# A hybrid encoder on one core: epsilon inside the sums of squares, a polish of two VectorE operations, one product per head norm, and another split of the last outputs

## The chip, the cores and the metric

The kernel runs on one core of a Trainium2 chip. The metric is the device time of one execution in microseconds: the median of three runs for the kernel before. The profile shows one further execution. Engines are named as in the profile: PE (TensorE matmul), DVE (VectorE), ACT (ScalarE), POOL (GpSimd), SP (the queue that issues DMAs).

## What is computed

One batch of 1024 tokens of width 1024 goes through four residual layers: attention (windowed heads of group A and full, RMS-normed heads of group B), an MLP, a spatial gating layer, an MLP, and a last RMSNorm. Every norm of it is of one kind, and those are what the change is about:

```python
def _rmsnorm(x, g):
    xf = x.astype(jnp.float32)
    y = xf * lax.rsqrt(jnp.mean(xf * xf, axis=-1, keepdims=True) + EPS)   # EPS = 1e-6
    return (y * g.astype(jnp.float32)).astype(x.dtype)

# group B of the attention layer: a norm over the 64 elements of a head
qb = _apply_axial_rope(_rmsnorm(qb, qn_g), cos_r, sin_r, cos_c, sin_c)
kb = _apply_axial_rope(_rmsnorm(kb, kn_g), cos_r, sin_r, cos_c, sin_c)
...
def _mlp(x, norm_g, w1, w2):
    h = _rmsnorm(x, norm_g)
    return x + jnp.square(jax.nn.relu(h @ w1)) @ w2
...
return _rmsnorm(h, final_norm)
```

## The kernel before

Activations lie transposed: 128 features on the partitions, tokens along the free axis, in two halves of 512 (`HN`). A tile `x[k][:, half]` is 128x512. Each fp32 product is three products of high and low parts (`mm3`, L268 to 270); the products of statistics (`ones`, `blk32`) are plain fp32 and show as two rows each. Both MLPs use a scheme of seven products for four (`product`, `up_step`), whose partial sums are put together from the PSUM banks by DVE (`r`, `u`, `ub`, `ua`).

A norm goes in four steps. ACT squares each x tile and POOL adds the squares up (`add_sq`, L311 to 314). PE adds over the partitions with a matrix of ones (`ssb`). ACT gives a first estimate of the inverse root: Ln and Exp (L321, L322) in the attention and the first MLP, one Abs_reciprocal_sqrt (L324) later. DVE polishes it by one Newton step: L325 makes the mean plus eps, L329 to L331 do the step. So a polish is four DVE operations. The activations are not scaled by it ahead of the products: `z` (L902) applies it to the finished `up` sums, and the attention applies it behind its projection.

The heads of group B have their own norm, inside `rotate` (L422 to 463), which is called for the key heads and for two sets of query heads, each for two halves: three normed calls a half, six in all. DVE does the four products of the rotation (L428, L430), ACT squares the two source banks (L433, L434), POOL subtracts and adds (L435, L436). The rest is a generator, `chain`, put into the list `chains`. `tick()` advances each generator of the list by one `yield`, and `lin`, the input projection, calls it after each k step, that is after twelve products. In the chain PE adds the squares over each head with two products by `blk32` (tile `hss`), DVE makes `ha` (L448), ACT does Ln and Exp into `hy`, DVE polishes with three operations (L329 to L331) and scales the rotated heads (L456), which are then split and stored to DRAM (`qs`, L461).

The last norm (`final`) runs for the whole first half, and for the second half in two quarters of 256 tokens, `rest` set. In the second half the last tile of x to be finished is x[3]: its `dz` products come last, DVE adds them (L1087), and `done` squares the tile (L1000). Each of the eight output tiles of a quarter is either scaled on DVE in one operation (L1113), or on ACT by the weight (L1110) and on POOL by rstd (L1111). Every third tile (`k % 3 == 2`: tiles 2 and 5) goes the second way. SP issues the output DMAs in the order of k.

A scheduler sets the order on each engine from the order in which the program emits its instructions, with pins (`in_turn`) that keep some behind the last product. Tiles of 128x512 come from a ring of twelve buffers (`tr` and `nr`, pool `trp`); a tile's first writer waits for the last reader of the tile that had the buffer before. PSUM has eight banks (`psp`).

Of the kernel before, what the change touches and what calls it, by code (L numbers as in the profile page):

```python
# [7 lines left out]
F32 = mybir.dt.float32  # L8
# [5 lines left out]
P = 128  # L14
# [18 lines left out]
def tile_kernel(ctx: ExitStack, tc: tile.TileContext, I, out, upto=99, dbg=None):  # L33
# [54 lines left out]
    par = const("par", [P, N_PAR])  # L88
    eps = cp.tile([P, 1], F32, name="eps")
    dve.memset(eps, EPS)  # L90
    ones = cp.tile([P, P], F32, name="ones")
# [213 lines left out]
    def add_sq(k, half, xs, w_=HN):  # L305
        if (half, "n") not in sumsq:
            a = nr("ss")
            act.activation(a[:, 0:w_], xs, AF.Square)
            sumsq[half, "n"] = 1
            sumsq[half] = a  # L310
        else:  # L311
            t = tr("sq")[:, 0:w_]
            act.activation(t, xs, AF.Square)  # L313
            pool.tensor_tensor(sumsq[half][:, 0:w_], sumsq[half][:, 0:w_], t, op=ALU.add)  # L314

    rsq = ["exp"]

    def rsqrt0(y0, a, s, scale):

        if rsq[0] == "exp":  # L320
            act.activation(y0, s, AF.Ln, scale=scale, bias=eps)  # L321
            act.activation(y0, y0, AF.Exp, scale=-0.5)  # L322
        else:
            act.activation(y0, s, AF.Abs_reciprocal_sqrt, scale=scale, bias=eps)  # L324
        dve.tensor_scalar(a, s, scale, EPS, op0=ALU.mult, op1=ALU.add)  # L325

    def newton(y0, a, dst):

        dve.tensor_tensor(a, y0, a, op=ALU.mult)  # L329
        dve.scalar_tensor_tensor(a, a, -0.5, y0, op0=ALU.mult, op1=ALU.mult)  # L330
        dve.scalar_tensor_tensor(dst, a, 1.5, y0, op0=ALU.add, op1=ALU.mult)  # L331

    def rstd_rows(half):

        s = ps("ssb")
        mm(s, ones, sumsq[half], True, True)
        y0, a = tr("y0"), tr("va")
        rsqrt0(y0, a, s, 1.0 / D)
        r = nr("rstd")
        newton(y0, a, r)  # L340
        return r

    def rstd_cols(half):

        s = ps("ssc")
        for tb in range(4):
            mm(s[:, tb : tb + 1], sumsq[half][:, tb * P : (tb + 1) * P], ones[:, 0:1], True, True)
        y0, a = sm("rc_y", [P, 4]), sm("rc_a", [P, 4])
        rsqrt0(y0, a, s[:, 0:4], 1.0 / D)
        r = sm("rc_r", [P, 4])  # L350
        newton(y0, a, r)
        return r
# [57 lines left out]
    def att_rstd(half):  # L410
# [4 lines left out]
        rsqrt0(y0, a, s, 1.0 / D)  # L415
        dve.tensor_scalar(evb[:, half], s, EPS / D, EPS * EPS, op0=ALU.mult, op1=ALU.add)
        rst[half] = rstb[:, half]
        newton(y0, a, rst[half])

    ready = {}  # L420

    def rotate(key, half, p1, p2, C, S, c1=None, c2=None, late=0):  # L422
# [8 lines left out]
        if c1 is not None:  # L431
            s1, s2 = tr("s1"), tr("s2")
            act.activation(s1, p1, AF.Square)  # L433
            act.activation(s2, p2, AF.Square)  # L434
        pool.tensor_tensor(de[:, 0], de[:, 0], w1, op=ALU.subtract)  # L435
        pool.tensor_tensor(de[:, 1], de[:, 1], w2, op=ALU.add)  # L436

        def chain():
            for _ in range(1 + late):
                yield 1  # L440
            if c1 is not None:
                s = ps("hss")
                mm(s, blk32, s1, True, False)
                mm(s, blk32, s2, False, True)
                yield 1
                y0, a = tr("hy"), tr("ha")

                dve.scalar_tensor_tensor(a, s, 1.0 / 64.0, evb[:, half], op0=ALU.mult, op1=ALU.add)  # L448
                act.activation(y0, a, AF.Ln)
                act.activation(y0, y0, AF.Exp, scale=-0.5)  # L450
                yield 1
                newton(y0, a, a)
                if key == "k":
# [638 lines left out]
    def final(half, a, b, rest):  # L1092
# [11 lines left out]
        r = nr("rstd")[:, 0:w_]  # L1104
        newton(y0, va, r)
        for k in range(KT):
            xs = x[k][:, half, a:b]
            o = tr("o")[:, 0:w_]
            if k % 3 == 2:
                act.activation(o, xs, AF.Copy, scale=col(C_FIN + k))  # L1110
# [266 lines left out]
```

## Time and profile before

| | us |
|---|---|
| median of 3 runs (lowest to highest) | 2071.59 (2068.70 to 2072.35) |
| the profiled execution | 2072.43 |
| its span from first to last instruction | 2070.7 |
| PE busy in it | 2027.1 (98%) |
| DVE busy | 1457.3 (70%) |
| ACT busy | 961.8 (46%) |
| POOL busy | 568.6 (27%) |

A row of a timeline gives the start and the length in us of one instruction or of several of a kind in a run (x6: six), its engine, the line, what it writes and reads, and in brackets how long the engine stood idle just ahead of it and which instruction ended that. Instructions in a pipeline overlap a little, so a row can be longer than the step to the next one. A releaser is inferred from the semaphores; of several it is the one that came last.

### The profile page before, as it was taken

The page shows a single profiled execution, that of the slowest core. Times are in us where ns is not written, and L with a number is a line of the kernel's source. Part 1 is how long each engine was busy: PE and PEld are TensorE (multiplying, and loading weights), DVE is VectorE, ACT ScalarE, POOL GpSimd, SP SyncE. Part 2 cuts the span into 40 slices and gives each one's busy share as a digit, 9 for nine tenths or more (in the row PEclk, how much of TensorE's full clock was granted, in tenths as well). Part 3 has the DMA queues.
Part 4 walks back from the last instruction along what each step waited for, and adds up shares of the span by engine and source line. Part 5 has one row for each costly group of instructions (what it writes and reads, how often), then busy time and mean ns, then how long its engine had stood idle before and what let it go on. Part 6 is the DMA issues. An engine that isn't in the chain of part 4 may idle for free.

```text
span 2070.7 us, 27136 instructions
## 1 busy us (share of the span) xinstructions
PE 2027.1 (98%) x9162; PEld 1672.5 (81%) x9162; DVE 1457.3 (70%) x2322; ACT 961.8 (46%) x1765; POOL 568.6 (27%) x440
## 2 busy tenths in 40 slices
PE   8998999999999999999999999999999999999997
PEld 7786877788878888888888888888788888888886
DVE  6878878855796666766696545646976767846976
ACT  5525767763543333435444444533533334544542
POOL 4324565642232222200002125423132223000012
PEclk9999999999999999999999999999999999999998
DMA  4354121134135444767364310342154446856543
GB/s 163 128 183 137 39 70 33 45 112 145 59 132 168 148 158 159 264 218 287 126 215 141 103 60 11 107 146 104 66 180 148 155 152 209 296 212 204 163 141 109
DMA packets 207307, 294.92 MB, mean 142 GB/s; under 512 B 19648, under 2 KB 88768, under 8 KB 207168
## 3 DMA queue, kind: packets, MB, share of 16 engines
q1 hardware_dynamic: 207168, 293.19, 42.9%
q8 instruction: 72, 1.18, 0.2%
q14 instruction: 67, 0.55, 0.1%
HBM read 207.13 MB, written 85.98 MB: 142 GB/s over the span
## 4 chain that ended last, share of the span: by engine, by line
PE 85%; DVE 9%; issue 2%; ACT 2%; POOL 1%; DMA 0%; DVEq 0%; SPq 0%; POOLq 0%; ACTq 0%
PE up L72 26%; PE lin L72 17%; PE dy L72 16%; PE dx L72 13%; PE av L72 4%; PE st L72 3%; PE mx L72 1%; PE vp L72 1%; DVE mb L603 1%; DVE w L147 1%; PE kp L72 1%; DVE rec L691 1%; DVE pp L643 1%; PE bc L72 1%; PE hss L72 1%
## 5 line engine op out<-in xcount | busy, mean ns | idle before, releaser
L72 PE MATMUL up<-h,w 128*128 128x512 f32 x1536 | 363.1, 389 | 5.4 <-ACT w L146 3.0
L72 PE MATMUL dy<-w,w 128*128 128x512 f32 x1488 | 353.8, 389 | 0.0
L72 PEld LDWEIGHTS up<-h,w 128*128 128x128 f32 x1536 | 288.1, 188 | 66.1 <-ACT w L146 3.4
L72 PEld LDWEIGHTS dy<-w,w 128*128 128x128 f32 x1488 | 279.3, 188 | 58.4 <-issue 0.5
L314 POOL TENSOR_TENSOR ss<-ss,sq 128x512 f32<-128x512 f32 x69 | 106.9, 1551 | 669.6 <-ACT sq L313 574.5
L72 PE MATMUL dx<-w,w 128*128 128x512 f32 x1152 | 276.7, 389 | 0.0
L72 PE MATMUL up<-w,w 128*128 128x512 f32 x1152 | 276.6, 390 | 0.0
L72 PEld LDWEIGHTS up<-w,w 128*128 128x128 f32 x1152 | 216.2, 188 | 45.8 <-ACT h L835 0.5
L72 PEld LDWEIGHTS dx<-w,w 128*128 128x128 f32 x1152 | 216.2, 188 | 44.9
L146 ACT CAST w<-wr 128x512 fp32r<-128x512 f32 x288 | 167.5, 620 | 144.7 <-DVE wr L179 39.0
L147 DVE TENSOR_TENSOR w<-wr,w 128x512 fp32r<-128x512 f32 x288 | 201.4, 709 | 23.9 <-ACT w L146 20.0
L72 PE MATMUL lin<-h,w 128*128 128x512 f32 x768 | 181.3, 393 | 1.1 <-POOL w L123 0.6
L72 PEld LDWEIGHTS lin<-h,w 128*128 128x128 f32 x768 | 143.3, 188 | 33.6 <-issue 2.4
L956 POOL TENSOR_TENSOR t<-ua,ub 128x512 f32<-128x512 f32 x32 | 44.8, 1398 | 452.8 <-ACT ua L903 431.4
L645 POOL TENSOR_TENSOR pp<-pe,pp 128x512 fp32r<-128x512 f32 x107 | 143.1, 1361 | 77.6 <-ACT pp L641 55.3
L147 DVE TENSOR_TENSOR w<-ur,w 128x512 fp32r<-128x512 f32 x224 | 156.0, 706 | 6.3 <-ACT w L146 6.3
L146 ACT CAST w<-ur 128x512 fp32r<-128x512 f32 x224 | 135.9, 620 | 40.9 <-DVE w L147 18.5
L147 DVE TENSOR_TENSOR w<-ws,w 128x512 fp32r<-128x512 f32 x128 | 94.0, 735 | 68.0 <-ACT w L146 67.5
L72 PE MATMUL st<-r,k 128*128 128x512 f32 (+2 forms) x384 | 132.2, 402 | 4.6 <-DVE mb L603 3.7
L146 ACT CAST w<-ws 128x512 fp32r<-128x512 f32 x128 | 79.5, 621 | 111.6 <-DVE ws L226 75.5
L903 ACT ACTIVATE ua<-ua 128x512 f32<-128x512 f32 x64 | 40.5, 633 | 172.8 <-DVE ua L902 172.7
L902 DVE SCALAR_TENSOR_TENSOR ua<-up,rstd 128x512 f32<-128x512 f32 x32 | 22.0, 688 | 129.0 <-PE up L72 129.0
(195 smaller groups left out, 3151.1 us busy)
## 6 DMA issues: line engine op xcount, KB each, us to landing
ur<-ucd SPq DMA_DIRECT2D x224, 256.0 KB, 3.6
wr<-in_w SPq DMA_DIRECT2D x256, 128.0 KB, 2.7
ucd<-t SPq DMA_DIRECT2D x128, 256.0 KB, 2.0
wr<-in_w SPq DMA_DIRECT2D x128, 256.0 KB, 3.7
ucd<-ub SPq DMA_DIRECT2D x64, 256.0 KB, 2.0
x<-in_xT SPq DMA_DIRECT2D x32, 256.0 KB, 3.4
xmd<-x SPq DMA_DIRECT2D x32, 256.0 KB, 2.1
ucd<-ua SPq DMA_DIRECT2D x32, 256.0 KB, 2.0
```

What stands on the lines that cost most here:

```text
L72: last_mm[0] = pe.matmul(o, l, r, start=start, stop=stop, **kw)
L146: act.copy(w[:, 0], src)
L147: dve.tensor_tensor(w[:, 1], src, f(w[:, 0]), op=ALU.subtract)
L314: pool.tensor_tensor(sumsq[half][:, 0:w_], sumsq[half][:, 0:w_], t, op=ALU.add)
L603: dve.tensor_reduce(M[n][:, tb, kh : kh + 1], p_, axis=AX.X, op=ALU.max)
L643: dve.tensor_copy(pp[:, 0], e)
L645: lo.tensor_tensor(pp[:, 1], e, f(pp[:, 0]), op=ALU.subtract)
L691: dve.scalar_tensor_tensor(y, den, 2.0, y, op0=ALU.subtract, op1=ALU.mult)
L902: dve.scalar_tensor_tensor(dst, src, 0.0, r[half], op0=ALU.max, op1=ALU.mult)
L903: act.activation(dst, dst, AF.Square)
L956: pool.tensor_tensor(t3, ua[:, 1], ub[:, 1], op=ALU.subtract)
```

## The change

Four edits. (1) The constant tile `eps` and its use as a bias are gone. POOL adds EPS * D / P to each sum of squares once, behind the second of its terms; over 128 partitions that makes EPS * D, and with the scale 1/D the mean has EPS. The term EPS * EPS in `evb` falls away. (2) `rsqrt0` lets ACT square the estimate (`q`), and `newton` is two operations: q times the sum (read from PSUM) times -0.5 and the scale, then plus 1.5 times the estimate. The head norms do the same, with one tile more (`hq`). (3) In `rotate` POOL adds the two squares, so that one product by `blk32` is left for a head norm, and one more `yield` stands ahead of it. (4) In the second half, tiles 1, 3, 4, 6 and 7 of the first quarter and 1, 3 and 6 of the last one are scaled by ACT and POOL, instead of 2 and 5.

```diff
-    eps = cp.tile([P, 1], F32, name="eps")
-    dve.memset(eps, EPS)
...
-            pool.tensor_tensor(sumsq[half][:, 0:w_], sumsq[half][:, 0:w_], t, op=ALU.add)
+            acc = sumsq[half][:, 0:w_]
+            pool.tensor_tensor(acc, acc, t, op=ALU.add)
+            sumsq[half, "n"] += 1
+            if sumsq[half, "n"] == 2:
+
+                pool.tensor_scalar(acc, acc, EPS * D / P, None, op0=ALU.add)
...
-            act.activation(y0, s, AF.Ln, scale=scale, bias=eps)
+            act.activation(y0, s, AF.Ln, scale=scale)
             act.activation(y0, y0, AF.Exp, scale=-0.5)
         else:
-            act.activation(y0, s, AF.Abs_reciprocal_sqrt, scale=scale, bias=eps)
-        dve.tensor_scalar(a, s, scale, EPS, op0=ALU.mult, op1=ALU.add)
-
-    def newton(y0, a, dst):
-
-        dve.tensor_tensor(a, y0, a, op=ALU.mult)
-        dve.scalar_tensor_tensor(a, a, -0.5, y0, op0=ALU.mult, op1=ALU.mult)
-        dve.scalar_tensor_tensor(dst, a, 1.5, y0, op0=ALU.add, op1=ALU.mult)
+            act.activation(y0, s, AF.Abs_reciprocal_sqrt, scale=scale)
+        act.activation(q, y0, AF.Square)
+
+    def newton(y0, q, s, scale, dst):
+
+        dve.scalar_tensor_tensor(q, s, -0.5 * scale, q, op0=ALU.mult, op1=ALU.mult)
+        dve.scalar_tensor_tensor(dst, q, 1.5, y0, op0=ALU.add, op1=ALU.mult)
...
-        dve.tensor_scalar(evb[:, half], s, EPS / D, EPS * EPS, op0=ALU.mult, op1=ALU.add)
+        dve.tensor_scalar(evb[:, half], s, EPS / D, None, op0=ALU.mult)
...
             act.activation(s2, p2, AF.Square)
+            pool.tensor_tensor(s1, s1, s2, op=ALU.add)
...
             if c1 is not None:
+                yield 1
                 s = ps("hss")
-                mm(s, blk32, s1, True, False)
-                mm(s, blk32, s2, False, True)
+                mm(s, blk32, s1, True, True)
                 yield 1
-                y0, a = tr("hy"), tr("ha")
+                y0, a, q = tr("hy"), tr("ha"), tr("hq")
...
                 act.activation(y0, y0, AF.Exp, scale=-0.5)
+                act.activation(q, y0, AF.Square)
                 yield 1
-                newton(y0, a, a)
+                newton(y0, q, a, 1.0, a)
...
+        others = () if not rest else (1, 3, 4, 6, 7) if b < HN else (1, 3, 6)
         for k in range(KT):
...
-            if k % 3 == 2:
+            if k % 3 == 2 if not rest else k in others:
                 act.activation(o, xs, AF.Copy, scale=col(C_FIN + k))
                 pool.tensor_tensor(o, o, r, op=ALU.mult)
```

In the order of the compiled program three places change. On PE, in the second half's projection, the products of the two query norms (`hss`) stand among those of `lin`, and before it reads:

```order
173 L72 MATMUL hss_1176<-s_188_1121,blk_200 128x512
174 L72 MATMUL hss_1176<-s_189_1122,blk_200 128x512
175 L72 MATMUL lin_1148<-h_124,w_962 128x512 x3
176 L72 MATMUL lin_1149<-h_124,w_962 128x512 x3
177 L72 MATMUL lin_1150<-h_124,w_962 128x512 x3
178 L72 MATMUL lin_1151<-h_124,w_962 128x512 x3
179 L72 MATMUL hss_1196<-s_193_1134,blk_200 128x512
180 L72 MATMUL hss_1196<-s_194_1135,blk_200 128x512
```

After, on PE at the same place, and on POOL what feeds it (`de` is the rotated pair, `s` the squares):

```order
170 L72 MATMUL lin_1151<-h_123,w_962 128x512 x3
171 L72 MATMUL lin_1152<-h_123,w_962 128x512 x3
172 L72 MATMUL lin_1153<-h_123,w_962 128x512 x3
173 L72 MATMUL hss_1190<-s_192_1121,blk_199 128x512
174 L72 MATMUL lin_1150<-h_141,w_967 128x512 x3
...
178 L72 MATMUL hss_1211<-s_197_1135,blk_199 128x512
```

```order
49 L438 TENSOR_TENSOR de_1114<-de_1114,w_190_1115 128x512
50 L439 TENSOR_TENSOR de_1114<-de_1114,w_191_1116 128x512
51 L437 TENSOR_TENSOR s_192_1121<-s_192_1121,s_193_1122 128x512
52 L438 TENSOR_TENSOR de_1128<-de_1128,w_195_1129 128x512
53 L439 TENSOR_TENSOR de_1128<-de_1128,w_196_1130 128x512
54 L437 TENSOR_TENSOR s_197_1135<-s_197_1135,s_198_1136 128x512
```

The products of a norm stand one k step of `lin` later (behind those with w_962), and POOL adds the squares as the third of its operations for a pair of heads. Counted in products of `lin` from the start of the projection's rotated part, the six norms stood behind 0, 64, 120, 132, 216 and 228, and stand behind 0, 59, 132, 144, 228 and 240.

On DVE at the start of the first MLP (`va` and `rstd` are the two norms, `ua` and `ub` the first activations, `r` and `u` sums of banks, `w` and `wr` weights), before:

```order
702 L325 TENSOR_SCALAR va_5495<-ssb_5492 128x512
703 L329 TENSOR_TENSOR va_5495<-y_1323_5494,va_5495 128x512
704 L330 SCALAR_TENSOR_TENSOR va_5495<-va_5495,y_1323_5494 128x512
705 L331 SCALAR_TENSOR_TENSOR rstd_5499<-va_5495,y_1323_5494 128x512
706 L325 TENSOR_SCALAR va_5506<-ssb_5503 128x512
707 L902 SCALAR_TENSOR_TENSOR ua_5514<-up_5286,rstd_5499 128x512
708 L329 TENSOR_TENSOR va_5506<-y_1327_5505,va_5506 128x512
...
715 L941 SCALAR_TENSOR_TENSOR ub_5554<-up_5541,u_1333_5534 128x512
```

And after, the same engine and place:

```order
686 L332 SCALAR_TENSOR_TENSOR va_5499<-ssb_5496,va_5499 128x512
687 L333 SCALAR_TENSOR_TENSOR rstd_5503<-va_5499,y_1329_5498 128x512
688 L906 SCALAR_TENSOR_TENSOR ua_5516<-up_5290,rstd_5503 128x512
689 L940 TENSOR_TENSOR r_1293_5303<-up_5523,r_1293_5303 128x512
690 L145 TENSOR_TENSOR w_5520<-wr_4573,w_5520 128x512
691 L332 SCALAR_TENSOR_TENSOR va_5509<-ssb_5506,va_5509 128x512
692 L145 TENSOR_TENSOR w_5540<-wr_4637,w_5540 128x512
693 L333 SCALAR_TENSOR_TENSOR rstd_5513<-va_5509,y_1333_5508 128x512
694 L941 TENSOR_TENSOR u_1339_5536<-up_5483,r_1293_5303 128x512
695 L177 TENSOR_TENSOR wr_4637<-wr_4637,wr_4913 128x512
696 L945 SCALAR_TENSOR_TENSOR ub_5556<-up_5543,u_1339_5536 128x512
```

From the first row on `va` to the one on `ub` there were fifteen rows and are eleven: the four polish operations gone, and one weight combination (L177) moved ahead of `ub`. In the second MLP the same stretch goes from fifteen to ten rows, with its L179 moved behind `ub`.

On DVE at the end of the program (`o` are the outputs of the second half's two quarters, `dz` the last products), before:

```order
2271 L330 SCALAR_TENSOR_TENSOR va_18082<-va_18082,y_3361_18081 128x256
2272 L331 SCALAR_TENSOR_TENSOR rstd_18091<-va_18082,y_3361_18081 128x256
2273 L1113 SCALAR_TENSOR_TENSOR o_18095<-x_16408,par,rstd_18091 128x256
2274 L1113 SCALAR_TENSOR_TENSOR o_18098<-x_16410,par,rstd_18091 128x256
...
2278 L1113 SCALAR_TENSOR_TENSOR o_18136<-x_16422,par,rstd_18091 128x256
2279 L1087 TENSOR_TENSOR x_16414<-dz_18065,x_16414 128x256
2280 L325 TENSOR_SCALAR va_18158<-ssb_18154 128x256
```

And after:

```order
2235 L332 SCALAR_TENSOR_TENSOR va_18083<-ssb_18079,va_18083 128x256
2236 L333 SCALAR_TENSOR_TENSOR rstd_18092<-va_18083,y_3367_18082 128x256
2237 L1119 SCALAR_TENSOR_TENSOR o_18095<-x_16408,par,rstd_18092 128x256
2238 L1119 SCALAR_TENSOR_TENSOR o_18108<-x_16412,par,rstd_18092 128x256
2239 L1119 SCALAR_TENSOR_TENSOR o_18125<-x_16418,par,rstd_18092 128x256
2240 L1091 TENSOR_TENSOR x_16414<-dz_18066,x_16414 128x256
2241 L332 SCALAR_TENSOR_TENSOR va_18161<-ssb_18157,va_18161 128x256
2242 L333 SCALAR_TENSOR_TENSOR rstd_18164<-va_18161,y_3380_18160 128x256
```

The addition to x[3] (L1091) stands behind three outputs instead of six.

## Rows read from the trace of the kernel before

**Rows 1.** The page's part 4: the chain of waits by engine.

```profile
PE 85%; DVE 9%; issue 2%; ACT 2%; POOL 1%; DMA 0%; DVEq 0%; SPq 0%; POOLq 0%; ACTq 0%
```

**Rows 2.** Chain of waits, pieces in order of time: start us, length us, what.

```profile
118.95 2.76 PE lin L72 x12
121.71 1.72 PE hss L72 x4
```

**Rows 3.** Timeline of PE in the input projection (columns as described above).

```profile
66.02 4.37 PE L72 MATMUL lin<-h,w 128*128 128x512 f32 x18 [0.55 <-POOL w L123]
70.67 6.19 PE L72 MATMUL lin<-h,w 128*128 128x512 f32 x26 [0.28 <-DVE w L123]
77.23 1.98 PE L72 MATMUL hss<-s,blk 128*128 128x512 f32 x4 [0.37 <-ACT s L433]
...
91.79 1.88 PE L72 MATMUL hss<-s,blk 128*128 128x512 f32 x4
...
117.07 1.88 PE L72 MATMUL hss<-s,blk 128*128 128x512 f32 x4
...
121.55 1.88 PE L72 MATMUL hss<-s,blk 128*128 128x512 f32 x4
```

**Rows 4.** Timeline of POOL: rotations behind the second key norm and query norms.

```profile
77.28 1.27 POOL L436 TENSOR_TENSOR de<-de,w 128x512 f32<-128x512 f32 x1 [0.25 <-DVE de L430]
...
91.56 1.28 POOL L436 TENSOR_TENSOR de<-de,w 128x512 f32<-128x512 f32 x1 [1.95 <-DVE de L430]
...
114.91 1.30 POOL L435 TENSOR_TENSOR de<-de,w 128x512 f32<-128x512 f32 x1 [3.76 <-DVE de L430]
...
118.86 1.68 POOL L436 TENSOR_TENSOR de<-de,w 128x512 f32<-128x512 f32 x1
```

**Rows 5.** Timelines of ACT, DVE and PE at the first MLP's start.

```profile
569.79 0.63 ACT L322 ACTIVATE y<-y 128x512 f32<-128x512 f32 x1
...
570.84 0.68 DVE L325 TENSOR_SCALAR va<-ssb 128x512 f32<-128x512 f32 x1
...
579.09 0.68 DVE L941 SCALAR_TENSOR_TENSOR ub<-up,u 128x512 f32<-128x512 f32 x1
...
574.69 2.88 PE L72 MATMUL up<-w,w 128*128 128x512 f32 x12
579.92 1.39 PE L72 MATMUL up<-h,w 128*128 128x512 f32 x5 [2.35 <-DVE ub L941]
```

**Rows 6.** Timelines of ACT, DVE and PE at the second MLP's start.

```profile
1467.94 1.27 ACT L324 ACTIVATE y<-ssb,eps 128x512 f32<-128x512 f32 x2
...
1468.66 0.69 DVE L325 TENSOR_SCALAR va<-ssb 128x512 f32<-128x512 f32 x1 [0.28 <-ACT y L324]
1469.39 0.69 DVE L329 TENSOR_TENSOR va<-y,va 128x512 f32<-128x512 f32 x1
...
1477.33 0.68 DVE L941 SCALAR_TENSOR_TENSOR ub<-up,u 128x512 f32<-128x512 f32 x1
...
1478.16 1.16 PE L72 MATMUL up<-h,w 128*128 128x512 f32 x4 [3.01 <-ACT w L146]
```

**Rows 7.** Timelines of DVE, POOL and PE at the end; last, a window's row.

```profile
2055.55 3.43 DVE L1113 SCALAR_TENSOR_TENSOR o<-x,par,rstd 128x256 f32<-128x256 f32 x6
2058.91 0.41 DVE L1087 TENSOR_TENSOR x<-dz,x 128x256 f32<-128x256 f32 x1
...
2063.47 3.40 DVE L1113 SCALAR_TENSOR_TENSOR o<-x,par,rstd 128x256 f32<-128x256 f32 x6
...
2055.65 1.86 POOL L1111 TENSOR_TENSOR o<-o,rstd 128x256 f32<-128x256 f32 x2 [6.44 <-DVE rstd L331]
...
2052.51 0.59 PE L72 MATMUL ssb<-sq,ones 128*128 128x256 f32 x2
...
2059.82 1.14 PE L72 MATMUL ssb<-sq,ones 128*128 128x256 f32 x2 [1.97 <-ACT sq L1000]
...
2059.80:2061.00 1.20, 1.14 (x2) 0.42 (x2) 0.00 (x0) 0.01 (x1) 0.00 (x0) 0.55 0.84 282
```

A window's row gives its bounds and length, the busy us of PE, PEld, DVE, ACT and POOL, PE's granted clock, the share of the DMA engines and GB/s.

More of the change, by code (lines that the diff above doesn't have):

```diff
@@ L313, in add_sq, with rsqrt0 @@
             act.activation(t, xs, AF.Square)
-            pool.tensor_tensor(sumsq[half][:, 0:w_], sumsq[half][:, 0:w_], t, op=ALU.add)
+            acc = sumsq[half][:, 0:w_]
[3 more added lines that the diff above has]
+                pool.tensor_scalar(acc, acc, EPS * D / P, None, op0=ALU.add)
     rsq = ["exp"]
-    def rsqrt0(y0, a, s, scale):
+    def rsqrt0(y0, q, s, scale):
         if rsq[0] == "exp":
-            act.activation(y0, s, AF.Ln, scale=scale, bias=eps)
+            act.activation(y0, s, AF.Ln, scale=scale)
             act.activation(y0, y0, AF.Exp, scale=-0.5)
         else:
-            act.activation(y0, s, AF.Abs_reciprocal_sqrt, scale=scale, bias=eps)
-        dve.tensor_scalar(a, s, scale, EPS, op0=ALU.mult, op1=ALU.add)
-    def newton(y0, a, dst):
-        dve.tensor_tensor(a, y0, a, op=ALU.mult)
-        dve.scalar_tensor_tensor(a, a, -0.5, y0, op0=ALU.mult, op1=ALU.mult)
-        dve.scalar_tensor_tensor(dst, a, 1.5, y0, op0=ALU.add, op1=ALU.mult)
+            act.activation(y0, s, AF.Abs_reciprocal_sqrt, scale=scale)
[3 more added lines that the diff above has]
+        dve.scalar_tensor_tensor(dst, q, 1.5, y0, op0=ALU.add, op1=ALU.mult)
     def rstd_rows(half):
@@ L339, in rstd_rows @@
         r = nr("rstd")
-        newton(y0, a, r)
+        newton(y0, a, s, 1.0 / D, r)
         return r
@@ L350, in rstd_cols @@
         r = sm("rc_r", [P, 4])
-        newton(y0, a, r)
+        newton(y0, a, s[:, 0:4], 1.0 / D, r)
         return r
@@ L415, in att_rstd @@
         rsqrt0(y0, a, s, 1.0 / D)
-        dve.tensor_scalar(evb[:, half], s, EPS / D, EPS * EPS, op0=ALU.mult, op1=ALU.add)
+        dve.tensor_scalar(evb[:, half], s, EPS / D, None, op0=ALU.mult)
         rst[half] = rstb[:, half]
-        newton(y0, a, rst[half])
+        newton(y0, a, s, 1.0 / D, rst[half])
     ready = {}
@@ L1104, in final @@
         r = nr("rstd")[:, 0:w_]
-        newton(y0, va, r)
+        newton(y0, va, s, 1.0 / D, r)
+        others = () if not rest else (1, 3, 4, 6, 7) if b < HN else (1, 3, 6)
         for k in range(KT):
```

## The prediction

> **What bounds the kernel now.** I began with the chain of waits by engine [rows 1]: PE makes 85% of it and DVE 9%, so a DVE operation counts only where PE stands still for it, and a PE product nearly always. The next views were the timelines, searched for such places near each edited line. There are four. In the input projection PE itself does the head norms' products [rows 2, 3]. At the start of each MLP it stands 2.35 and 3.01 us until the first `up` bank is free [rows 5, 6]. At the end nothing is left to fill PE, and each step of the last norm is on the path [rows 7]. The second MLP row names the ACT cast of a weight as releaser; that had long been done, and in the program the product also needs the bank that DVE L941 reads, which runs 1477.33 to 1478.01. So it is the same wait as in the first MLP.
>
> **Norm sums.** The ten POOL additions of eps stand after the first of seven additions to each sum, whose last addends come much later, and two sums end in the final norm. So they cost nothing: in the trace PE never waits for a sum on POOL, and each is read behind a row of products. The memset and the bias that go are outside the path.
>
> **Head norms (57 to 160 us): -4.4.** A product of a statistic costs PE 0.86 us: a pair takes 1.72 [rows 2]. Six of twelve go: 6 x 0.86 = -5.16. Two waits of `lin` on split weights, 0.55 and 0.28, and the 0.37 in front of the second key norm [rows 3] go with it if the order holds, -1.20 (the casts move ahead of the norm's DVE work).
> The price is a POOL addition, and the order puts it third, behind the two additions of the rotation, so the square's sum is ready 1.3 us behind them [rows 4]. One more step of `lin` stands ahead, worth 2.76 us [rows 2]. For the first query norm of half 1: POOL starts at 114.91 and now does three, 3 x 1.3, ready at 118.8; four products saved so far shift that by 3.44 to 115.4. PE came at 117.07, less 3.44, plus 2.76: 116.4. No wait, 1.0 of slack. The second: 118.86 + 1.68 + 2 x 1.3 for the two sums, less 3.44, is 119.7; PE at 121.55 - 4.30 + 2.76 = 120.0. Slack 0.3. Half 0 by the same count: 91.56 + 1.28 + 1.3 - 1.72 = 92.4 against 91.79 - 1.72 + 2.76 = 92.8; its second about even.
> The second key norm is the tight one. There the order shows 59 products of `lin` ahead where there were 64, so the added step gives no cover. PE arrives at 77.23 - 0.37 - 0.86 - 0.83 - 5 x 0.23 = 74.0. The rotation's POOL work ended at 77.28 + 1.27 = 78.55 and the sum then at 79.85, if nothing upstream moves: a wait of 5.8, the upper bound. But DVE's queue between the two key norms loses three 512-wide operations and two small ones, about 2.7 us with their stretch, and starts 0.7 earlier, with perhaps 0.4 less stretch beside POOL: ready at about 76.05. I take 2.0 us, the lower bound is none. Sum: -5.16 - 1.20 + 2.0 = -4.4, between -6.4 and -0.6.
> What the attention then loads from DRAM is stored by these same chains, so its start moves with them.
>
> **First MLP (566 to 580): -1.7.** DVE runs without a gap: from the first L325 to L941 are 15 operations, 570.84 to 579.09 [rows 5], which is 0.59 a step (8.25 / 14); a step that needs the one before takes 0.73 (1468.66 to 1469.39 in [rows 6]). Now eleven stand there: two polishes of two, `ua`, `r`, `u`, three weight subtractions and `ub`. ACT has a Square more behind the first Exp (569.79 + 0.63; at the same length the Square ends at 571.1), so the first polish begins at about 571.15 instead of 570.84. Ten steps, two of them dependent: 571.15 + 2 x 0.73 + 8 x 0.60 = 577.4, against 579.09: -1.7. PE waits 2.35, so all of it shows. Bounds: -2.35 and 0. The zero end: DVE now reads the statistic's PSUM bank in the polish itself, so the bank comes free later. PE took it at 574.69 [rows 5]; the second polish ends its first step at 574.4 to 575.1, so 0.4 of a wait may appear ahead of the big one, and is swallowed by it.
>
> **Second MLP (1464 to 1479): -2.4.** L325 starts at 1468.66 and L941 at 1477.33 [rows 6], again 15 operations. Here the first estimate is one ACT instruction (L324 x2, 1.27); the Square between puts the first polish at 1469.35 (+0.69). Then nine steps to `ub`, since the order moves a weight combination (L179) behind it: 1469.35 + 0.73 + 8 x 0.60 = 1474.9, against 1477.33. -2.4 of the 3.01 that PE waits; bounds -3.0 and 0.
> In the SGU layer's start PE has other work, and its norms stay off the path.
>
> **Tail (2050 to 2070.7): -2.3.** Rows 7 give the chain: quarter A's rstd, its six DVE outputs (2055.55, 3.43 us), the last DVE addition to x (2058.91), ACT's square, PE's sum at 2059.82, the rstd of B, its outputs from 2063.47, and the end 3.83 behind DVE's last. Quarter A: four DVE steps become ACT's Square and two, so rstd ends one step (0.41, as L1087) sooner, at 2055.1 instead of just ahead of 2055.55. DVE then has three outputs, not six; beside POOL each takes about 0.9 (POOL holds 1.86 / 2 = 0.93 each and now works through), alone 0.4. They end near 2057.3, and the addition comes at 2057.4, 1.5 sooner. Square 2057.9, PE 2058.4; that sum took 1.14 us at a granted clock of 0.55 (mostly the 1.2 GHz level) after PE had idled 1.97 us, where the quarter before took 0.59 straight behind products; the idle time now is near 1 us, and it may be 0.6 to 1.14. So ACT has the estimate at 2059.4 to 2060.0. But ACT's new Square for B writes a buffer of the ring of twelve that A's rstd used, and its fifth POOL product ends 5 x 0.93 behind 2055.2, at about 2059.9. So Square 2059.95 to 2060.4, two DVE operations to 2061.35; before, rstd ended just ahead of 2063.47. -2.05. The outputs give 0.25 more, because the second comes from POOL 1.1 behind rstd instead of from DVE at 1.4. Sum -2.3. Bounds: -3.2 with nothing held by POOL and the high clock; +0.5 if a POOL product beside DVE takes 1.5 us: five of them from 2055.2 hold the Square until 2062.7, and rstd ends at 2064.1.
> Here a rule speaks against the change. The Trainium skill, "GPSIMD Engine Reference" (opening and section 1), calls GpSimd the wrong choice for elementwise arithmetic, about two times slower than VectorE, with SBUF interfaces shared. The trace agrees on the ratio: 0.93 against 0.40 alone, and DVE's outputs slow beside it. By it the tail would be +0.5 and the sum -8.0.
>
> **Sum.** -4.4 - 1.7 - 2.4 - 2.3 = -10.8. The profiled execution was 2072.43 (span 2070.7, 1.73 around it), 0.84 above the median of 2071.59; the sum is a difference, so it is taken from the median: 2060.8.
>
> **Rivals.** (1) POOL's sums are late: the 79.85 holds at the second key norm, so the projection gives only -0.6. For it speaks POOL's queue and the missing cover; against it DVE's lighter queue. -0.6 - 1.7 - 2.4 - 2.3 = -7.0: 2064.6. (2) The MLPs keep their waits, since the Squares and the held banks eat what DVE saves: -4.4 - 2.3 = -6.7: 2064.9. Against: DVE ran back to back there. (3) POOL makes the tail longer (+0.5): -8.0, 2063.6. (4) Two or three of these together: (1) and (2) give -2.9, 2068.7, no difference that could be told. (5) Slower: POOL's sum stalls PE at all six head norms. It must lose more than 5.16 + 1.20 + 6.4 (the other three places) + 4.1 = 16.9 us to be told as a loss; 5.8 at the key norm and then over 2.2 at each of the five others, whose counted slack is 0 to 1.0. A POOL addition stretched to 1.68 costs 0.4 apiece, so this needs a DVE queue that also falls behind: about 2076 to 2078. (6) The change doesn't do what it says: the Square on ACT, at 0.63 like Exp, only replaces a DVE step of 0.69 in each chain. Then chains without a DVE backlog gain nothing, and the MLPs, with a backlog, still do; this is inside (2).
>
> **How the numbers follow.** Chances: forecast 0.62, (1) 0.14, (2) with (6) 0.08, (3) 0.06, (4) 0.06, (5) 0.04. A change under 0.2% (4.1 us) can't be told from none: faster is below 2067.45. Faster: 0.62 + 0.14 + 0.08 + 0.06 less some edges = 0.87; same 0.09; slower 0.04. All lower bounds together give -6.4 - 2.35 - 3.0 - 3.2 = -15, 2056.6. The range takes that end and on the other side rivals (1) to (3) with a microsecond and a half: 2056.6 to 2066.5.
>
> **What would show it.** In the changed profile: six products of `hss`, PE's wait in front of the second of them near 2 us and none over 0.5 at the others; PE's waits for `ub` at about 0.65 and 0.6 us; DVE's last addition to x about 1.5 us sooner against the end of `dz`, and ACT's Square in the last quarter released by POOL. The forecast is wrong if PE waits over 4 us on POOL, if the `up` waits stay above 2, or if quarter B's rstd follows the end of `dz` by as much as before.

## The result, and the profile after

The changed kernel takes 2057.01 us (four runs, 2056.32 to 2057.21) against 2070.94 us of the kernel before beside it (2068.70 to 2072.35): a ratio of 0.9928, 95% interval 0.9915 to 0.9940. That is 14 to 15 us, where 10.8 were forecast: the direction and the places were right, the size was too small. The median lies inside the forecast range of 2056.6 to 2066.5; the ratio, which makes 2056.0 of 2070.94, lies just beyond its low end. The profiled execution has a span of 2054.5 us, 16.2 less than the one of before.

The chain of waits by engine, page of the changed kernel, answers [rows 1]: DVE's part fell from 9% to 7%.

```profile
PE 86%; DVE 7%; ACT 2%; issue 2%; POOL 1%; DMA 1%; DVEq 0%; SPq 0%; POOLq 0%; ACTq 0%
```

PE's timeline in the input projection (start, length, idle time ahead and releaser), to be laid beside [rows 3]; the last row is the first product of the attention's scores, which began at 148.01 before.

```profile
56.18 1.02 PE L72 MATMUL hss<-s,blk 128*128 128x512 f32 x2
...
58.70 13.71 PE L72 MATMUL lin<-h,w 128*128 128x512 f32 x59
73.41 1.13 PE L72 MATMUL hss<-s,blk 128*128 128x512 f32 x2 [1.00 <-POOL s L437]
...
118.13 1.02 PE L72 MATMUL hss<-s,blk 128*128 128x512 f32 x2
...
141.01 1.07 PE L72 MATMUL mx<-k,r 128*128 128x512 f32 x4
```

And POOL's sum for the second of them, beside [rows 4]:

```profile
70.83 1.30 POOL L439 TENSOR_TENSOR de<-de,w 128x512 f32<-128x512 f32 x1 [0.24 <-ACT s L435]
72.08 1.27 POOL L437 TENSOR_TENSOR s<-s,s 128x512 f32<-128x512 f32 x1
```

Each `hss` is one product (the other three read like the last), the two waits on weights are gone (59 products of `lin` in one row without idle time), and a single wait of 1.00 us for POOL's sum is left. From the first head norm to the first score it took 148.01 - 57.30 = 90.71 and takes 141.01 - 56.18 = 84.83 us: -5.88.

PE and DVE at the start of the two MLPs, beside [rows 5, 6]:

```profile
565.54 2.88 PE L72 MATMUL up<-w,w 128*128 128x512 f32 x12
569.02 2.98 PE L72 MATMUL up<-h,w 128*128 128x512 f32 x12 [0.60 <-ACT w L144]
...
568.19 0.68 DVE L945 SCALAR_TENSOR_TENSOR ub<-up,u 128x512 f32<-128x512 f32 x1
...
1459.06 3.06 PE L72 MATMUL up<-h,w 128*128 128x512 f32 x12 [0.40 <-DVE va L332]
1461.96 2.88 PE L72 MATMUL up<-w,w 128*128 128x512 f32 x12
1464.68 3.01 PE L72 MATMUL up<-h,w 128*128 128x512 f32 x12
...
1463.85 0.68 DVE L945 SCALAR_TENSOR_TENSOR ub<-up,u 128x512 f32<-128x512 f32 x1
```

The first wait fell from 2.35 to 0.60 us (-1.75). In the second MLP it is gone (3.01 us less, and 5.89 to 2.72 between the two rows of products); a wait of 0.40 for the statistic's bank came ahead of it, so the second MLP gains 2.6.

The tail, DVE, POOL, ACT and PE, beside [rows 7]:

```profile
2041.55 2.24 DVE L1119 SCALAR_TENSOR_TENSOR o<-x,par,rstd 128x256 f32<-128x256 f32 x3
2044.01 0.42 DVE L1091 TENSOR_TENSOR x<-dz,x 128x256 f32<-128x256 f32 x1 [0.22 <-PE dz L72]
...
2047.58 3.47 DVE L1119 SCALAR_TENSOR_TENSOR o<-x,par,rstd 128x256 f32<-128x256 f32 x5
...
2041.65 4.10 POOL L1117 TENSOR_TENSOR o<-o,rstd 128x256 f32<-128x256 f32 x5 [5.88 <-ACT o L1116]
...
2046.14 0.42 ACT L328 ACTIVATE va<-y 128x256 f32<-128x256 f32 x1
...
2039.32 4.65 PE L72 MATMUL dz<-w,w 128*128 128x256 f32 x36
...
2044.93 0.70 PE L72 MATMUL ssb<-sq,ones 128*128 128x256 f32 x2 [0.53 <-ACT sq L1004]
```

DVE's last addition to x now waits for PE's `dz`, not PE for DVE. PE idles 0.53 us, and the last sum takes 0.70 instead of 1.14 us (the first experiment shows that this sum takes 0.70 in an execution without any edit too). POOL's five products end at 2045.75, before ACT's Square at 2046.14, so the Square was not held by them. From the start of the last `dz` (2052.76 before, 2039.32 now) to the end of the span: 17.94 before, 15.18 now, -2.76.

The four places together give -5.88 - 1.75 - 2.6 - 2.76 = -13.0. The spans differ by 16.2. Of the rest, 1.1 us lie ahead of the first head norm (57.30 against 56.18), and 2.2 between the scores' start and 198 us, where the profile before has a low clock. A granted clock of 1.00 is PE's level of 2.4 GHz, 0.50 that of 1.2 GHz; a value between is a window with both. Windows of both (bounds, length, busy us of PE, PEld, DVE, ACT, POOL, granted clock, DMA share, GB/s), first before, then after at the corresponding stretch:

```profile
180.00:184.00 4.00, 4.00 (x13) 3.32 (x12) 3.03 (x5) 0.60 (x1) 1.04 (x1) 0.50 1.04 323
184.00:188.00 4.00, 4.00 (x15) 3.17 (x14) 3.44 (x6) 3.39 (x7) 1.29 (x1) 0.75 1.05 227
```

```profile
172.00:176.00 4.00, 3.60 (x18) 3.06 (x19) 3.94 (x7) 1.42 (x3) 2.04 (x2) 1.00 1.02 349
176.00:180.00 4.00, 4.00 (x19) 3.32 (x18) 3.97 (x6) 3.97 (x9) 2.59 (x2) 1.00 1.05 241
```

At half the clock PE does 13 instead of 19 products in 4 us.

### The profile page after: what moved, and what is told of

It reads as the page before. It is cut to its first block, busy times and chain, and to the rows that moved or that the text cites. A ratio compares the mean times of both kernels' runs of the same rounds, so it can differ in the third digit from the quotient of the medians.

```text
span 2054.5 us, 27119 instructions
## 1 busy us (share of the span) xinstructions
PE 2017.2 (98%) x9150; PEld 1667.3 (81%) x9150; DVE 1435.3 (70%) x2281; ACT 971.1 (47%) x1790; POOL 594.6 (29%) x460
## 4 chain that ended last, share of the span: by engine, by line
PE 86%; DVE 7%; ACT 2%; issue 2%; POOL 1%; DMA 1%; DVEq 0%; SPq 0%; POOLq 0%; ACTq 0%
PE up L72 27%; PE lin L72 17%; PE dy L72 16%; PE dx L72 13%; PE av L72 4%; PE st L72 3%; PE mx L72 1%; PE vp L72 1%; PE kp L72 1%; DVE mb L607 1%; DVE w L145 1%; DVE rec L695 1%; PE dz L72 1%; PE bc L72 1%; DVE pp L647 0%
## 5 line engine op out<-in xcount | busy, mean ns | idle before, releaser
L72 PE MATMUL av<-pp,v 128*128 128x512 f32 x384 | 108.4, 393 | 4.4 <-POOL pp L649 1.8
```

Source lines behind the costliest of these rows:

```text
L72: last_mm[0] = pe.matmul(o, l, r, start=start, stop=stop, **kw)
```

## The experiments

**The kernel before, once more** (no edit).

> The kernel before, unchanged, for a second profile. Two theories on the 2.2 us that the changed kernel gained between the first score products and the rows at 198 us, where the profile before has a granted clock of 0.50 to 0.75 from 179 to 187 us and the profile after has 1.00. Theory A (chance): the lower clock there belongs to that execution; this profile shows 1.00 there or not, run by run, and where it shows 1.00 the span is about 2.2 us shorter (2068.5). Theory B (order): the kernel before always has it, since PE waits 0.95, 1.60 and 0.69 us just ahead; this profile shows 0.50 to 0.75 again and a span near 2070.7. The ratio is 1.000 in both.

Ratio 0.9998 (0.9989 to 1.0007), but the profiled execution has a span of 2066.7, 4.0 us less than the first. Three places make it up. The first head norm comes at 56.00 instead of 57.30 (1.3). The low clock is there, as theory B had it, but shorter (0.74 and 0.50 from 172 to 176, 0.90 to 178), and from the first score to the first MLP's statistic (`ssb`) it takes 417.23 instead of 419.48 us (2.25), as in the changed kernel (417.30). And PE's last sum takes 0.70 us behind the same idle time for which the first profile has 1.14 (0.46 with what follows):

```profile
2056.28 0.70 PE L72 MATMUL ssb<-sq,ones 128*128 128x256 f32 x2 [1.97 <-ACT sq L1000]
```

So the 1.1 and the 2.2 us come and go from one execution to the next without an edit, and so does the higher clock of the last sum. Against this profile the tail gains 17.48 - 15.18 = 2.3 us, not 2.76; three more profiles with the old outputs and the old polish have 17.42 to 17.49.

**One product alone.**

```diff
             act.activation(s2, p2, AF.Square)
+            pool.tensor_tensor(s1, s1, s2, op=ALU.add)
...
+                yield 1
                 s = ps("hss")
-                mm(s, blk32, s1, True, False)
-                mm(s, blk32, s2, False, True)
+                mm(s, blk32, s1, True, True)
```

> Only the head norms' squares are added on POOL, with one product and one more yield; eps, the polish of four DVE operations and the outputs as before. Theory (terms add): six products fewer, -5.2, the two weight waits gone, -0.8, and a wait for the sum at the second key norm that is longer than the 1.0 us of the changed kernel, since DVE's polishes still stand ahead of the rotation: 2 to 3.5 us; -3 to -4.5 in all, 2066.5 to 2068, with another 2.2 if the clock does not fall at 170 to 190 us. Rival (POOL's queue alone decides): the wait at the second key norm is 5 to 5.8 us and the gain is under 1 us, 2070 to 2071.

Nothing: 1.0003 (0.9994 to 1.0012). PE, in the projection:

```profile
57.29 1.12 PE L72 MATMUL hss<-s,blk 128*128 128x512 f32 x2 [0.49 <-POOL s L435]
...
77.29 1.13 PE L72 MATMUL hss<-s,blk 128*128 128x512 f32 x2 [2.34 <-POOL s L435]
...
119.27 1.12 PE L72 MATMUL hss<-s,blk 128*128 128x512 f32 x2 [1.38 <-POOL s L435]
123.88 1.12 PE L72 MATMUL hss<-s,blk 128*128 128x512 f32 x2 [0.72 <-POOL s L435]
```

The waits for sums, 4.9 us, eat the 5.2 of the six products; from 57.29 to the first score at 147.02 it is 1.0 us less than before. The second key norm waits as the theory said, but the query norms of the second half wait too, where the count in the prediction had 0.3 to 1.0 us of slack. So this edit alone does not pay.

**Eps and the polish alone**: edits (1) and (2) of the change, with two products for a head norm and the outputs as before.

> Only eps in the sums and the polish of one Square and two DVE operations, for all norms; head norms keep two products, outputs as before. Theory: first MLP's wait for ub from 2.35 to about 0.6 (-1.75), second MLP's from 3.0 to 0 (-3.0), last norm two times 0.43 (-0.9), projection and attention as before: -5.6, about 2065.3. Rival (DVE's shorter queue also opens the projection): another -1.2 to -2 there, 2063.5.

2066.73, ratio 0.9970 (0.9957 to 0.9982). As the theory had it: both MLPs' waits for `ub` are gone from PE's timeline (the theory had 0.6 us left in the first), and no gain in the projection. From its first head norm to the first score it takes 92.75 us, 2.0 more than before: the six pairs of products stay, and `lin` waits 1.26 us for the bank of the statistic, which is now read later:

```profile
75.47 1.66 PE L72 MATMUL lin<-h,w 128*128 128x512 f32 x6 [1.26 <-DVE va L332]
```

**The outputs alone**: edit (4).

> Only the other split of the last outputs: tiles 1, 3, 4, 6, 7 of the first quarter and 1, 3, 6 of the last on ACT and POOL. Theory: DVE's last addition to x comes 1.2 to 1.5 us sooner (three outputs fewer ahead of it), PE's last sum runs at the higher clock (0.6 to 0.7 instead of 1.14 us), the outputs end 0 to 0.3 sooner against rstd: -1.7 to -2.3, span about 2068.5. Rival (POOL's products stretch DVE's): 0 to +0.5.

Ratio 0.9990 (0.9981 to 0.9999), some 2 us. Counted from the start of the last `dz`, DVE's last addition comes 1.2 us sooner (4.96 against 6.15 us), and the end 1.5 sooner than in the second profile of before (16.01 against 17.48). PE's sum took 0.70, as in that profile, so the theory's higher clock for it is no gain of this edit. No sign of a stretched tail.

The three alone add to +0.6 - 6.2 - 2.1 = -7.7 by their ratios; together they gave 14.7. Seven us are interaction, give or take some 3 by the intervals of these ratios. The profiles place it: from the first head norm to the first score one product alone gives -1.0, the polish alone +2.0, and the change -5.9, so 6.9 us lie in the projection.

**The changed kernel, once more.**

> The changed kernel, unchanged, for a second profile. The kernel before showed a granted clock of 0.50 for some 4 to 7 us between 172 and 187 us in both its profiles, the changed kernel none in its one. Theory A (chance): the dip comes in this one too, and the span is then 1.5 to 3 us longer than 2054.5. Theory B (the change removes it): clock 1.00 there again, span within 0.8 us of 2054.5.

Theory A. 2058.03, ratio 0.9931 (0.9916 to 0.9946); this profiled execution has a span of 2057.4, of whose 2.9 us more 1.0 lie ahead of the first head norm and 1.9 between the first score and the first MLP, and a dip of the clock:

```profile
172.00:176.00 4.00, 3.77 (x10) 2.67 (x11) 4.00 (x6) 0.00 (x0) 2.96 (x2) 0.50 1.04 375
176.00:180.00 4.00, 4.00 (x13) 3.19 (x12) 2.64 (x5) 2.41 (x4) 1.28 (x1) 0.57 1.02 252
```

**The change without its other split of the outputs.**

> The changed kernel with the outputs of the second half split as before (tiles 2 and 5). The other split alone gave about 2 us, so theory (it adds to the rest): 2 to 2.7 us slower than the changed kernel, 2059 to 2060, and still 12 us faster than before, though one product alone gave 0 and the polish alone 5.5. Rival (the parts simply add): 0 and 5.5, 2066.5.

2059.24, 0.9938 (0.9923 to 0.9952): 1.2 to 1.5 us slower than the change, a little under the expectation, and far from 2066.5. From the start of the last `dz` to the end it takes 16.49 us, 15.18 in the changed kernel: 1.3. The interaction is not in the tail.

**The change with the head norms polished by three DVE operations.**

```diff
-                y0, a, q = tr("hy"), tr("ha"), tr("hq")
+                y0, a = tr("hy"), tr("ha")
...
-                act.activation(q, y0, AF.Square)
                 yield 1
-                newton(y0, q, a, 1.0, a)
+                dve.tensor_tensor(a, y0, a, op=ALU.mult)
+                dve.scalar_tensor_tensor(a, a, -0.5, y0, op0=ALU.mult, op1=ALU.mult)
+                dve.scalar_tensor_tensor(a, a, 1.5, y0, op0=ALU.add, op1=ALU.mult)
```

> The changed kernel, with the head norms' polish by three DVE operations as before; the norms of the tokens keep Square and two operations. It tells which of the two shorter polishes lets the one product pay. Theory (the token norms' polish, which stands in DVE's queue ahead of the rotation of the second key half): the second key norm waits 1.0 to 1.6 us, the query norms 0 to 0.7, total 0.5 to 1.5 us slower than the changed kernel, 2057.5 to 2058.5. Rival (the head norms' own polish): the waits of one product alone come back, 1.4 and 0.7 us at the query norms of the second half, total 3 to 5 us slower, 2060 to 2062.

2062.84, 0.9955 (0.9939 to 0.9972): 4.8 us slower than the change, the size of the rival but not its place. The wait at the second key norm is 1.87 instead of 1.00, the last query norm waits 0.24, and the clock fell behind the longer wait. From this norm to the next one PE takes 19.86 us, 17.54 in the changed kernel, so the low clock costs more here than the wait itself:

```profile
74.03 1.94 PE L72 MATMUL hss<-s,blk 128*128 128x512 f32 x2 [1.87 <-POOL s L437]
```

```profile
72.00:76.00 4.00, 2.13 (x4) 0.93 (x4) 1.54 (x6) 2.76 (x12) 1.98 (x2) 0.78 0.88 322
76.00:80.00 4.00, 4.00 (x15) 3.20 (x15) 2.57 (x5) 2.29 (x4) 0.00 (x0) 0.80 0.01 2
```

**The change without the added step of `lin`.**

```diff
             if c1 is not None:
-                yield 1
                 s = ps("hss")
```

> The changed kernel without the added yield ahead of the one product. Theory (POOL's sum is the third of its operations and needs the step): each query norm comes 2.76 us sooner in PE's order with 0.3 to 1.0 us of slack, so PE waits 1.8 to 2.5 us at each of four, and the same or more at the keys: 6 to 10 us slower than the changed kernel, 2063 to 2067. Rival (the sums are early enough anyway, since DVE's queue is shorter): within 1 us.

2069.66, 0.9989 (0.9980 to 0.9999): 11.6 us slower than the change, more than either expected. PE waits 1.12, 0.55 and 4.68 us for sums, and 1.46 for a bank, and behind the 4.68 the clock fell to 0.50 from 120 to 124 us (a norm's product took 2.07 us there):

```profile
120.29 2.07 PE L72 MATMUL hss<-s,blk 128*128 128x512 f32 x2 [4.68 <-POOL s L437]
```

Without the step the one product costs more in waits than it saves.

**One product with the head norms' own polish**, the token norms as before: the first experiment plus the Square and two operations in `chain`.

> The kernel before with the one product per head norm and with the head norms' own polish of a Square and two DVE operations; the token norms, eps and outputs as before. One product alone gave nothing (PE waited 0.49, 2.34, 1.38 and 0.72 us for POOL's sums). Theory (either shorter DVE queue opens the sums, and the head norms' own polish the more, since the changed kernel lost 4.8 us without it): the waits at the query norms go, the second key norm waits 1.5 to 2.3, and the gain is 2.5 to 4 us, 2068 to 2069.5. Rival (the token norms' polish is needed as well): under 1 us of gain, 2071 to 2072.

Ratio 0.9986 (0.9977 to 0.9995), 2.9 us: the theory. The query norms don't wait; the key norms wait 0.48 and 1.45. The next wait shows: 1.48 us at the first score for a load of what the chains stored. And in this profile the clock fell behind both MLPs' waits, which neither profile of before shows:

```profile
572.00:576.00 4.00, 1.70 (x4) 1.44 (x5) 4.00 (x8) 1.22 (x3) 0.00 (x0) 0.75 0.00 0
576.00:580.00 4.00, 4.00 (x16) 3.17 (x16) 2.97 (x6) 1.60 (x3) 0.00 (x0) 0.82 0.35 131
...
1474.00:1478.00 4.00, 4.00 (x12) 3.14 (x13) 2.84 (x5) 2.24 (x4) 0.00 (x0) 0.64 0.25 92
```

That gives the price of such a fall. The waits are as long as before, and the same twelve products behind each take 1.5 us more; the first profile of before first, then this one:

```profile
579.92 3.00 PE L72 MATMUL up<-h,w 128*128 128x512 f32 x12 [2.35 <-DVE ub L941]
1478.16 2.97 PE L72 MATMUL up<-h,w 128*128 128x512 f32 x12 [3.01 <-ACT w L146]
```

```profile
574.30 4.45 PE L72 MATMUL up<-h,w 128*128 128x512 f32 x12 [2.36 <-DVE ub L944]
1473.98 4.49 PE L72 MATMUL up<-h,w 128*128 128x512 f32 x12 [3.03 <-ACT w L146]
```

It is not won back: from the first MLP's statistic to the second's it takes 898.90 us, 897.45 in both profiles of before, and from there to the last `dz` 589.45, 587.82 before. So a fall costs 1.45 us in the first MLP and 1.63 in the second. In the profile of one product alone it came behind the second wait only, and cost the same there (589.44).

**The squares added on DVE**: `pool.tensor_tensor(s1, s1, s2)` in `rotate` becomes `dve.tensor_tensor`.

> The changed kernel with the two squares added on DVE instead of POOL. Theory (POOL's queue, where the sum stands third, makes the 1.0 us wait at the second key norm): the sum takes 0.6 on DVE right behind the squares, the wait falls below 0.3, and the rest of DVE's queue moves by six times 0.6 off the path: 0 to 1 us faster. Rival (DVE is the engine that is late in the projection): new waits at the query norms or for the scaled heads, 1 to 4 us slower.

2056.47, 0.9925 (0.9912 to 0.9939), and no wait at any head norm. So the sum's place in POOL's queue made the 1.00 us. Whether it is faster was asked again, below.

**Filled waits in the attention**: products of a zero matrix ahead of the first grid head's products with the values.

```diff
+        if fill and kt == 0:
+            keep(4, True)
+            first = False
+        if fill and kt == 3:
+            keep(7)
...
             mm(o, b, pp[:, 0, c0 : c0 + w_], False, False)
+            if fill and kt == 3:
+                keep(3)
```

> The changed kernel with fourteen further products of a zero matrix, 4, 7 and 3 of them, ahead of the first grid head's first and fourth softmax products, in the places where PE stood 0.95, 1.60 and 0.69 us (they add zero to the same bank). Theory (PE's idle time at 165 to 173 us makes the granted clock fall to 0.50 there in most executions): no dip between 160 and 190 us in the profile, spans near 2054.5 in each run and a median 0.5 to 1.5 us below the changed kernel's, 2056 to 2057.5. Rival (the dip has another cause): the dip is there as often, and the fillers cost 0 to 1 us.

2057.06, 0.9929 (0.9917 to 0.9942), no difference, and the dip is there (0.74, 0.50 and 0.90 from 168 to 174 us). But the test missed its point: the first filler had to wait for the same bank,

```profile
168.30 1.53 PE L72 MATMUL av<-k,zeror 128*128 128x512 f32 x4 [0.94 <-DVE mb L609]
```

so PE had stood as long as ever when the clock fell. What makes this dip stays open.

**Two queues for the last outputs**: the odd tiles of the last quarter issued on ACT's DMA queue.

> The changed kernel with the odd tiles of the last quarter issued on ACT's DMA queue instead of SP's, to tell what ends the program. SP issues the eight outputs some 0.49 us apart and the span ends 2.9 us behind the last issue. Theory (SP's issue rate holds the last outputs): the last issue comes 0.3 to 0.6 us sooner and the span is shorter by as much. Rival (DVE's and POOL's scaling, 3.5 us, sets it): within 0.2 us.

2058.46, 0.9935 (0.9922 to 0.9947), not faster. An issue on ACT's queue waits for its output, and ACT's scaling of tile 6 stood behind it:

```profile
2051.81 0.51 ACT L1116 ACTIVATE o<-x,par 128x256 f32<-128x256 f32 x1 [3.26 <-DVE o L1119]
```

From the end of rstd to the end of the span it takes 7.3 us, 7.0 in the changed kernel. It does not tell whether SP's rate or the scaling sets the end, since the edit made a wait of its own.

**The kernel before, kept busy in the MLPs' waits**: the waits stay, PE doesn't idle in them.

```diff
                 product(banks[g, 5 if i == 3 else i], g, i, i == 3)
+                if i == 4 and not filled:
+                    filled.append(g)
+                    with in_turn():
+                        for t in range(9 if l == 0 else 12):
+                            mm(banks[g, 4], zeror, hc[4, 0][:, 0], False, t == (8 if l == 0 else 11), skip_group_check=True)
```

> The kernel before with 9 and 12 products of a zero matrix added to the bank of the product just made, in the two places where PE stood 2.35 and 3.01 us for ub in the MLPs. The waits for ub stay on DVE's side; PE is only kept busy. Theory (in many executions of the kernel before the clock falls behind these waits, which no term of the forecast had): no low clock at 570 to 585 and 1470 to 1490 us in the profile, mean granted clock per run 0.996 to 0.997 instead of mostly 0.995, and 1 to 2 us faster than the kernel before. Rival (the clock falls there as often, or costs nothing): within 0.4 us, or slower by the fillers' 0.2.

2069.66 against 2071.88 us of the kernel before beside it; the ratio is 0.9992 (0.9983 to 1.0001), so by time alone it is at the edge of what can be told, with means of 2070.51 and 2072.24, 1.7 apart. The clocks of the runs are clear: the mean granted clock is 0.997 in ten of eleven, where the kernel before has 0.995 in thirteen of fifteen. As nothing but the two waits was filled, this says that the kernel before lost its clock behind them in most runs, though neither of its two profiles caught that. The profile here shows the fillers and no low clock behind them:

```profile
574.39 2.26 PE L72 MATMUL up<-w,zeror 128*128 128x512 f32 x9
576.91 2.96 PE L72 MATMUL up<-h,w 128*128 128x512 f32 x12 [0.26 <-DVE ub L949]
```

```profile
572.00:576.00 4.00, 4.00 (x19) 3.27 (x18) 4.00 (x7) 0.62 (x1) 0.00 (x0) 1.00 0.17 66
...
1474.00:1478.00 4.00, 3.79 (x17) 2.81 (x16) 4.00 (x8) 2.29 (x4) 0.00 (x0) 1.00 0.00 0
```

So work that computes nothing makes the kernel before no slower, and by its means some 1.7 us faster. The kernel before says the same without any edit: of its 81 executions beside the experiments and in the first of them, the 56 with a mean clock of 0.995 took 2072.6 us on average, the 10 with 0.997 took 2070.1, and all of them 2072.1. The mean clock does not tell where it was low, and at one and the same mean clock executions differ by up to 3.5 us, so these means support the 1.7 and do not prove it.

**The change and the sum on DVE, side by side.**

> The changed kernel a third time, in the same call as the next, for a direct comparison: 2057 to 2058.2, mean granted clock 0.996 to 0.998.

> The changed kernel with the squares added on DVE, again, beside the changed kernel. Theory (the 1.0 us wait at the second key norm is gone and nothing else is late): 0.8 to 1.2 us below the changed kernel of this call. Rival (the gain of the first run was the clock's chance): within 0.4 us.

2057.56 (0.9929, 0.9917 to 0.9941) and 2057.83 (0.9930, 0.9917 to 0.9942): the rival, no difference. The wait moved. With POOL the second key norm waits 1.02 us and the first score 0.16 for its load; with DVE it reads

```profile
74.03 1.12 PE L72 MATMUL hss<-s,blk 128*128 128x512 f32 x2
...
142.52 1.16 PE L72 MATMUL mx<-k,r 128*128 128x512 f32 x4 [0.71 <-DMA r<-qs_b]
```

The projection has become short enough that the stored and reloaded heads are the next limit. No version here beats the changed kernel by more than can be told.

## Why the prediction came out as it did

**Bound and places: right.** All four places gained, each by the wait or the work that was named, and eps cost nothing that shows: POOL's sums of the token norms hold nobody up. The size was 3.9 us short (10.8 against some 14.7, the middle of the three ratios of the changed kernel, 0.9928, 0.9931 and 0.9929). Of that 1.5 us lie in the head norms, 0.25 in the MLPs, none in the tail, and the rest, some 2, is the clock.

**Head norms, -4.4 forecast, -5.88 measured: the step that was mis-sized is the second key norm's wait.** The sum there was to be ready at 76.05, 2.0 us behind PE. With 1.1 us off for the earlier start that is 74.9. It was ready by 73.35 and PE, 0.5 ahead of the estimate, waited 1.00. DVE's rotation got ahead by more than the three operations and the lighter stretch counted: three small operations on `v` that stood ahead of it stand behind, and the two scalings of the heads take half the time, now that POOL's split of a weight no longer runs beside them. Before and after:

```profile
65.73 2.49 DVE L456 TENSOR_TENSOR de<-de,ha 128x512 f32<-128x512 f32 x2 [0.71 <-ACT ha L454]
```

```profile
62.62 1.29 DVE L460 TENSOR_TENSOR de<-de,ha 128x512 f32<-128x512 f32 x2 [0.74 <-ACT ha L458]
```

The slack at the query norms (1.0, 0.3, even) held: none waits. But the reason given for it was incomplete. It was worked out from POOL's rows of before, as if only the product count moved; one product alone shows that without the shorter polish two of these four wait 1.38 and 0.72. Either of the two shorter polishes, that of the tokens' norms or that of the heads', takes these waits away but for 0.24 us. The shorter polish is a condition of this term, and the prediction named it for the key norm only.

**First MLP, -1.7 against -1.75**, and **second MLP, -2.4 against -2.6**: right. `ub` comes 2.56 us sooner behind the statistic in the second, a little more than the 2.4, and would have left a wait of some 0.4. That it shows none is because PE itself came 0.40 later: the wait for the statistic's bank, foreseen for the first MLP, where it didn't come, stands in the second. One reading was wrong without effect: from the first L325 to L941 the first MLP of before has fourteen operations, not fifteen (the section on the change says fifteen too), so 8.25 us are 0.63 a step. The sum went by steps of 0.60 and 0.73, which the trace has.

**Tail, -2.3 against -2.76 of the first profiles, but -2.3 against the second profile of before: the right size by luck.** The addition came 1.5 sooner, as worked out. Two other steps failed and nearly cancel. The Square was to be held by POOL's fifth product; five took 4.10 us, 0.82 each and not 0.93, and ended 0.4 ahead of it. And the sum of before was read as slow, 1.14 us, because PE had idled 1.97; with the same idle time it took 0.70 in the second profile, so there was hardly a clock to win. The rule of the Trainium skill ("GPSIMD Engine Reference", opening), GpSimd at half VectorE's pace, is true of the single operation (0.82 us against 0.41 of DVE's addition of this size), but POOL's products lie beside DVE's, and the outputs alone gained about 2 us. That rival fell.

**What had no term, and is the largest miss: the clock behind the MLPs' waits.** The first profile of before had a clock of 1.00 behind both waits, so the prediction priced them at their length and the clock behind them at nothing. Where it falls it costs 1.45 and 1.63 us more, 3.1 for both, and the change, which leaves 0.60 and 0.40 us of these waits, shows no fall there in its three profiles. How often it falls in the kernel before is known from the runs alone: filled waits gain 1.7 us by the means, and the executions of before with a high clock lie 2.0 under the mean. The four terms make 5.88 + 1.75 + 2.6 + 2.3 = 12.5, with 1.7 to 2.0 it is 14.2 to 14.5, and measured were 13.9 (medians) to 14.9 (ratio). This agrees; the average share of the clock stays an estimate, for the interval of the filled waits reaches none. The dip in the attention is another matter: it stands in every profile but the first of the changed kernel, for 3 to 10 us, and accounts for 2.2 of the 16.2 between the first two profiles, not for a lasting gain.

**Rivals.** Late sums (1) came in a weaker form with one product alone (2.34 us at the second key norm, not 5.8), and shrank to 1.00 with the shorter polish. Waits kept in the MLPs (2), a longer tail (3) and a loss at all norms (5) did not occur; nearest to the last is the run without the added step, 11.6 us worse than the change with waits at three of the six norms, and still not slower than the kernel before.

## What to carry to other kernels

Price a removed PE wait at more than its length where some executions show a low clock behind such a wait: read several profiles, or the mean clock of each run, before settling the term. A second profile of the unchanged kernel also tells which of its rows are the execution's and not the program's, as the 1.14 us of the last sum. When an edit moves work to another engine in front of PE, ask which other edit of the same change makes that engine's input early; alone it may give nothing, as the one product did, and a sum of single effects (7.7 here) can be half of the whole (14.7). After a gain, look for the next wait: here the load at the first score took back what the sum on DVE gave.

## What was not expected of the hardware

One and the same program had its granted clock low near 175 us for very different times, about 7 and 3 us in the two profiles of before, none, 10 and 3 us in three of the change, though PE's waits up to the fall agree to 0.02 us where two profiles of a program were laid side by side. What it cost did not follow its length: from the first score to the first MLP's statistic it took 419.48 and 417.23 us before, and 417.30, 419.17 and 417.31 in the change, so in these five profiles a fall of 3 us cost nothing against none, and one of 7 or 10 about 2 us.

Behind waits of 1.87, 2.36, 3.01, 3.03 and 4.68 us in the projection and the MLPs the clock also fell in some profiles, and behind 2.34, 2.35 and 3.01 in others it did not. With the two waits in the MLPs filled the mean clock of the runs rose from 0.995 to 0.997.

An issue on ACT's DMA queue held an ACT operation behind it for 3.26 us.
